# First layer's attention scores of two query tiles in one pass, with the rotary high-by-low products as 64-row halves

## The chip, the cores and the metric

The kernel runs on one core of a Trainium2 chip. Five engines work side by side from queues of their own: PE (TensorE, matrix products; PEld is its weight side), DVE (VectorE), ACT (ScalarE), POOL (GpSimd) and SP, which mostly issues DMAs. The metric is the device time of one execution in microseconds (us), lower is better.

## What is computed

The reference is a trunk of two layers over 1024 latent and 256 context tokens of width 1024. The first layer's mixer, the one of interest, is multi-head latent attention with 8 heads. A head's query and key have 128 plain and 64 rotary elements, and the rotary key is one for all heads:

```python
def _block_attention(q, k, v, scale):
    ...
    def step(qi):
        s = jnp.einsum('bqhgd,bkhd->bhgqk', qi, k).astype(jnp.float32) * scale
        p = jax.nn.softmax(s, axis=-1).astype(v.dtype)
        return jnp.einsum('bhgqk,bkhd->bqhd', p, v)

def _mla_mixer(h, hc, w_dq, q_norm, w_uq, w_dkv, kv_norm, w_ukv, w_o, need_ctx):
    ...
    q = _mla_q(h, w_dq, q_norm, w_uq, rows, cols)
    k, v = _mla_kv(h, w_dkv, kv_norm, w_ukv, rows, cols)
    kc, vc = _mla_kv(hc, w_dkv, kv_norm, w_ukv, None, None)
    k_all = jnp.concatenate([kc, k], 1)
    v_all = jnp.concatenate([vc, v], 1)
    out = _block_attention(q[:, :, :, None], k_all, v_all, scale) @ w_o
    if need_ctx:
        qc = _mla_q(hc, w_dq, q_norm, w_uq, None, None)
        out_c = _block_attention(qc[:, :, :, None], kc, vc, scale) @ w_o
```

A layer norm, a dense MLP, neighbourhood attention as the second layer's mixer and another MLP follow; the change does not touch them.

## The kernel before

Each fp32 operand of a matrix product is kept as two parts, a high one in fp32r (a copy rounded to that type) and a low one, the remainder. A product is then three passes: high by high, high by low and low by high (`mm3`, lines 66 to 68).

Tokens are handled in tiles of 128; tiles 0 and 1 are the context. The keys stand in three groups `GR`, of 256, 512 and 512 columns. `p1b` computes the queries of all heads and stores them in DRAM. For the rotary part (`pe`) a PE transpose gives the 64 rotary rows twice, one copy below the other; ACT copies both to `qst` as the high part (L382), and DVE replaces rows 64 to 127 by the low part (L383). The rotary key `ck[g][b][:, 2, :]` also holds its 64 rows twice (b = 0 high, b = 1 low).

`attn0` goes through heads, and in a head through 5 pairs of query tiles. `softmax(h, t, ...)` makes the scores of one tile: for each key group five products into one PSUM bank, of 512 or 256 columns. L468, L469 and L472 are the plain part, L470 the rotary high key against both query parts at once over 128 rows, and L471 the low key in the same way. Then DVE copies the bank to `p` with a running maximum (L473), takes the maximum (L476), ACT makes the exponential (L478), DVE the reciprocal (L479), and DVE (odd tiles) or POOL (even tiles) scales (L480). `pv` handles the pair before: four PE transposes of `p` per two key tiles (L491), a split into `th` (ACT, L54) and `tl` (DVE, L55), and six products into `po`, which DVE copies out (L499). Pair 0 is the context and has one key group; pairs 1 to 4 have three.

Between the pairs stand pieces of other work: the next two heads' keys and values (`pj`, `pv`, lines 66 to 68) and the modulation products of the second layer (L155), which multiply with a 32-column weight in four column parts of the array side by side. PSUM has 8 banks: three with the tag "u" (`po`, projections, modulation), three "d" (scores), two "t" (transposes).

The calls in the code are not the order on the engines: a scheduler reorders each engine's instructions when the program is built, within the dependencies; PE then runs them strictly in that order. `issue_after` and `mark` only say behind which product a piece may come.

Of the kernel before, what the change touches and what calls it, by code (L numbers as in the profile page):

```python
# [10 lines left out]
F32 = mybir.dt.float32  # L11
F32R = mybir.dt.float32r
AF = mybir.ActivationFunctionType
# [5 lines left out]
P = 128  # L19
# [22 lines left out]
class Trunk:  # L42
# [304 lines left out]
    def p1b(self):  # L347
# [6 lines left out]
        with tc.tile_pool(name="p1b", bufs=1, reuse_waits="tile") as sp:  # L354

            def pe(hg):
                h, lo = self.wload(a["wuqp"][hg], [P, 4, 256], f"p{hg}")
                for g, (o, n) in enumerate(GR):
                    qr = []
                    for i in range(n // P):  # L360
                        t = o // P + i
                        sl = slice(i * P, (i + 1) * P)
                        pp = self.bank("u", f"pp{hg}{t}", (P, 256))
                        ch, cl = self.cq[g]
                        for k in range(4):
                            self.mm3(pp, ch[:, k, sl], cl[:, k, sl], h[:, k, :], lo[:, k, :], k == 0, k == 3)
                        r = sp.tile([P, 4, 2, 64], F32, tag="qr", bufs=8, name=f"qr{hg}{t}")
                        if g == 0:
                            nc.scalar.copy(r[:, :, 0, :], pp.rearrange("p (a b) -> p a b", b=64))
                        else:  # L370
                            x = sp.tile([P, 4, 64], F32, tag="qx", bufs=2, name=f"qx{hg}{t}")
                            nc.scalar.copy(x.rearrange("p a b -> p (a b)"), pp)
                            self.rope(sp, r[:, :, 0, :], x, t - 2, 4)
                        nc.vector.tensor_copy(r[:, :, 1, :], r[:, :, 0, :])
                        qr.append(r.rearrange("p a d b -> p a (d b)"))
                    for hh in range(4):
                        pt = self.bank("t", f"qt{hg}{g}{hh}", (P, 4, P))
                        for i in range(n // P):
                            nc.tensor.transpose(pt[:, i, :], qr[i][:, hh, :], self.ident)
                        st = sp.tile([P, 512], F32R, tag="qst", bufs=2, name=f"qst{hg}{g}{hh}")  # L380
                        pf = pt.rearrange("p a b -> p (a b)")[:, 0:n]
                        nc.scalar.copy(st[:, 0:n], pf)  # L382
                        nc.vector.tensor_tensor(st[64:128, 0:n], pf[64:128, :], self.f(st[64:128, 0:n]),  # L383
                                                op=ALU.subtract)
                        nc.scalar.dma_start(self.qs[hg * 4 + hh][g], self.f(st[:, 0:n]))

            def nope(pr):
# [19 lines left out]
    def attn0(self):  # L407
        nc, tc, a = self.nc, self.tc, self.a
        self.od = [self.dp.tile([P, H0, 256], F32, name=f"od{i}") for i in range(5)]
        with ExitStack() as es:  # L410
# [41 lines left out]
                nc.sync.dma_start(self.f(s[:, 0:n]), self.qs[h][g])  # L452
                return q, s

            def softmax(h, t, q, kt, gks):

                g, off = grp_of(t)
                qq, qst = q
                sl = slice(off, off + P)
                st = sp.tile([P, 6], F32, tag="st", bufs=8, name=f"st{h}{t}")  # L460
                p = sp.tile([P, NTOK], F32, tag="p", bufs=5, name=f"p{h}{t}")
                for i, gk in enumerate(gks):
                    o0, n = GR[gk]
                    o = self.bank("d", f"s{h}{t}{gk}")[:, 0:n]
                    kh, kl = kt[gk]
                    ph, pl = (x[:, 2, :] for x in self.ck[gk])
                    mm = nc.tensor.matmul
                    mm(o, lhsT=qq[:, 0, sl], rhs=kh, start=True, stop=False)  # L468
                    mm(o, lhsT=qq[:, 0, sl], rhs=kl, start=False, stop=False)  # L469
                    mm(o, lhsT=qst[:, sl], rhs=ph, start=False, stop=False)  # L470
                    mm(o, lhsT=qst[:, sl], rhs=pl, start=False, stop=False)  # L471
                    self.mark = mm(o, lhsT=qq[:, 1, sl], rhs=kh, start=False, stop=True)  # L472
                    nc.vector.tensor_scalar(p[:, o0:o0 + n], o, 1.0, None, op0=ALU.mult, op1=ALU.max,  # L473
                                            accum_out=st[:, i:i + 1])
                m = len(gks)
                nc.vector.tensor_reduce(st[:, 3:4], st[:, 0:m], axis=AX, op=ALU.max, negate=True)  # L476
                n = sum(GR[gk][1] for gk in gks)
                nc.scalar.activation(p[:, 0:n], p[:, 0:n], AF.Exp, bias=st[:, 3:4], accum_out=st[:, 4:5])  # L478
                nc.vector.reciprocal(st[:, 5:6], st[:, 4:5])  # L479
                (nc.vector.tensor_scalar(p[:, 0:n], p[:, 0:n], st[:, 5:6], None, op0=ALU.mult) if t % 2 else nc.gpsimd.tensor_tensor(p[:, 0:n], p[:, 0:n], st[:, 5:6].broadcast_to([P, n]), op=ALU.mult))  # L480
                return p

            def pv(h, h2, pair, ps_, nb, vs):
                po = self.bank("u", f"po{h}{pair}", (P, 256))
# [21 lines left out]
            for h in range(H0):  # L506
# [10 lines left out]
                    total = len(todo)  # L517
                qs_ = [load_q(h, g) for g in range(3)]
                for pair in range(5):
                    pl = [softmax(h, t, qs_[grp_of(t)[0]], ks[h2], [0] if pair == 0 else [0, 1, 2])  # L520
                          for t in (pair * 2, pair * 2 + 1)]
                    if pend is not None:
                        pv(*pend)
                    pend = (h, h2, pair, pl, 2 if pair == 0 else 10, vs)
# [916 lines left out]
```

## Time and profile before

| what | value |
|---|---|
| median of 3 runs | 3142.84 us (3138.31 to 3143.91) |
| time of the profiled execution | 3141.2 us |
| its span, first to last instruction | 3139.4 us |
| mean granted clock of TensorE | 0.984 of full speed |
| PE busy | 96% of the span |
| DVE, ACT, POOL busy | 57%, 39%, 34% |
| first layer's attention | about 265 to 747 us of the span |

Times in the views are us from the start of the span. A row of the timeline has the start, the length, the engine, the line of the kernel, the operation, output<-inputs and the shape; [x <- y] is idle time of the engine just before and what ended it. PE's records overlap, since products are pipelined: how fast it goes is read from the distance between two starts. Repeated instructions are merged into one row (x8).

### The profile page before, as it was taken

The page shows a single profiled execution, that of the slowest core. Times are in us where ns is not written, and L with a number is a line of the kernel's source. Part 1 is how long each engine was busy: PE and PEld are TensorE (multiplying, and loading weights), DVE is VectorE, ACT ScalarE, POOL GpSimd, SP SyncE. Part 2 cuts the span into 40 slices and gives each one's busy share as a digit, 9 for nine tenths or more (in the row PEclk, how much of TensorE's full clock was granted, in tenths as well). Part 3 has the DMA queues.
Part 4 walks back from the last instruction along what each step waited for, and adds up shares of the span by engine and source line. Part 5 has one row for each costly group of instructions (what it writes and reads, how often), then busy time and mean ns, then how long its engine had stood idle before and what let it go on. Part 6 is the DMA issues. An engine that isn't in the chain of part 4 may idle for free.

```text
span 3139.4 us, 42125 instructions
## 1 busy us (share of the span) xinstructions
PE 3023.0 (96%) x15894; PEld 2528.9 (81%) x15894; DVE 1776.4 (57%) x3619; ACT 1208.8 (39%) x2068; POOL 1077.1 (34%) x667
## 2 busy tenths in 40 slices
PE   8999999999989999999999999999988899999997
PEld 4798888888878888888887788888877788878886
DVE  4345665665656656422228777777757666632228
ACT  2234444444445444301002455555543555521101
POOL 3362111112124343462118522232324044455227
PEclk9999999999999999999999999999999999999998
DMA  8445333313524444774435111111124244476434
GB/s 331 157 153 185 127 114 113 122 35 99 180 77 157 149 148 141 261 248 148 133 114 183 66 46 45 43 45 46 39 82 163 103 157 163 165 271 231 145 114 168
DMA packets 205724, 429.22 MB, mean 137 GB/s; under 512 B 16896, under 2 KB 124544, under 8 KB 199760
## 3 DMA queue, kind: packets, MB, share of 16 engines
q1 hardware_dynamic: 151472, 296.97, 28.7%
q10 hardware_dynamic: 54048, 129.56, 10.5%
q8 instruction: 125, 2.05, 0.3%
q14 instruction: 79, 0.65, 0.1%
HBM read 298.50 MB, written 127.96 MB: 136 GB/s over the span
## 4 chain that ended last, share of the span: by engine, by line
PE 79%; DVE 7%; issue 5%; POOL 3%; DMA 3%; ACT 3%; SPq 0%; DVEq 0%; ACTq 0%; POOLq 0%
PE py L66 7%; PE py L67 7%; PE py L68 7%; PE nj L66 3%; PE nj L68 3%; PE nj L67 3%; PE sb L68 2%; PE sb L66 2%; PE sb L67 2%; PE pt L491 2%; PE sa L66 2%; PE mps L155 2%; PE sa L68 2%; PE sa L67 2%; PE sc L67 2%
## 5 line engine op out<-in xcount | busy, mean ns | idle before, releaser
L1085 DVE TENSOR_TENSOR y<-py,y 128x512 f32<-128x512 f32 x252 | 172.8, 690 | 443.7 <-PE py L68 443.7
L480 POOL TENSOR_TENSOR p<-p,st 128x1280 f32<-128x1280 f32 (+1 forms) x40 | 79.2, 1980 | 383.4 <-DVE st L479 277.8
L66 PE MATMUL nj<-hTa,whn 128*128 128x512 f32 (+1 forms) x512 | 201.4, 393 | 2.6 <-ACT njt L1125 2.6
L66 PE MATMUL py<-w2xh,ub 128*128 128x512 f32 x504 | 196.1, 389 | 0.0
L67 PE MATMUL py<-w2xl,ub 128*128 128x512 f32 x504 | 196.1, 389 | 0.0
L68 PE MATMUL py<-w2xh,ub 128*128 128x512 f32 x504 | 196.1, 389 | 0.0
L68 PE MATMUL nj<-hTa,wln 128*128 128x512 f32 (+1 forms) x512 | 189.2, 370 | 2.0 <-POOL wln L61 2.0
L67 PE MATMUL nj<-hTa,whn 128*128 128x512 f32 (+1 forms) x512 | 188.7, 369 | 0.0
L54 ACT CAST th<-pt 128x512 fp32r<-128x512 f32 x168 | 96.9, 586 | 164.7 <-PE pt L491 162.3
L473 DVE TENSOR_SCALAR_CACHE_REDUCE p<-s 128x512 f32<-128x512 f32 (+1 forms) x208 | 116.9, 584 | 60.2 <-PE pt L491 33.4
L55 DVE TENSOR_TENSOR tl<-pt,th 128x512 fp32r<-128x512 f32 x168 | 114.2, 687 | 61.0 <-ACT th L54 59.8
L61 POOL TENSOR_TENSOR wln<-rawn,whn 128x1024 fp32r<-128x1024 f32 x28 | 67.4, 2407 | 210.6 <-ACT whn L59 210.5
L1202 ACT ACTIVATE pp<-pp,nst 128x640 f32<-128x640 f32 (+1 forms) x128 | 102.9, 804 | 95.2 <-DVE nst L1200 94.8
L59 ACT CAST w2xh<-w2r 128x1024 fp32r<-128x1024 f32 x28 | 28.1, 1049 | 284.2 <-PE py L68 189.2
L66 PE MATMUL py<-w2th,ub 128*128 128x512 f32 x324 | 126.7, 392 | 4.1 <-DVE y L1083 4.1
L68 PE MATMUL py<-w2th,ub 128*128 128x512 f32 x324 | 127.7, 394 | 0.0
L67 PE MATMUL py<-w2wl,ub 128*128 128x512 f32 x324 | 127.0, 392 | 0.0
L66 PE MATMUL py<-w2wh,ub 128*128 128x512 f32 x324 | 127.0, 392 | 0.0
L67 PE MATMUL py<-w2tl,ub 128*128 128x512 f32 x324 | 126.8, 391 | 0.0
L68 PE MATMUL py<-w2wh,ub 128*128 128x512 f32 x324 | 126.8, 391 | 0.0
L61 POOL TENSOR_TENSOR w2xl<-w2r,w2xh 128x1024 fp32r<-128x1024 f32 x28 | 67.2, 2420 | 172.9 <-ACT w2xh L59 172.9
L66 PE MATMUL py<-woh,oh 128*128 128x512 f32 x288 | 115.8, 403 | 10.2 <-DVE ty L671 9.1
(2133 smaller groups left out, 9508.3 us busy)
## 6 DMA issues: line engine op xcount, KB each, us to landing
ub<-ud SPq DMA_DIRECT2D x288, 256.0 KB
adaw<-in_ada_w SPq DMA_DIRECT2D x40, 1024.0 KB
w1r<-in_w SPq DMA_DIRECT2D x64, 512.0 KB
w2r<-in_mlp_w SPq DMA_DIRECT2D x64, 512.0 KB
ud<-uhld ACTq DMA_DIRECT2D x29, 512.0 KB
ud<-uhlc ACTq DMA_DIRECT2D x29, 512.0 KB
ud<-uhlb ACTq DMA_DIRECT2D x29, 512.0 KB
ud<-uhla ACTq DMA_DIRECT2D x28, 512.0 KB
```

What stands on the lines that cost most here:

```text
L54: nc.scalar.copy(hi, ps)
L55: nc.vector.tensor_tensor(lo, ps, self.f(hi), op=ALU.subtract)
L61: return h, e.tensor_tensor(lo, src, self.f(hi), op=ALU.subtract)
L66: mm(out, lhsT=ah, rhs=bh, start=first, stop=False, skip_group_check=more)
L67: mm(out, lhsT=ah, rhs=bl, start=False, stop=False, skip_group_check=more)
L68: return mm(out, lhsT=al, rhs=bh, start=False, stop=last, skip_group_check=more)
L155: nc.tensor.matmul(ps[32 * j:32 * j + 32, :], lhsT=self.sT[:, k, :], rhs=x, start=(k == 0), stop=(k == KD - 1), tile_position=(0, 32 * j))
L473: nc.vector.tensor_scalar(p[:, o0:o0 + n], o, 1.0, None, op0=ALU.mult, op1=ALU.max, accum_out=st[:, i:i + 1])
L480: (nc.vector.tensor_scalar(p[:, 0:n], p[:, 0:n], st[:, 5:6], None, op0=ALU.mult) if t % 2 else nc.gpsimd.tensor_tensor(p[:, 0:n], p[:, 0:n ...
L491: nc.tensor.transpose(pt[:, c, i, :], ps_[i][:, col:col + P], self.ident)
L1085: self.mark = nc.vector.tensor_tensor(y[t][:, ns], py, y[t][:, ns], op=ALU.add)
L1202: nc.scalar.activation(pp[:, 0:n], pp[:, 0:n], AF.Exp, bias=st[:, 2:3], accum_out=st[:, 3:4])
```

## The change

Four things are done. The scores of both tiles of a pair are made in one call, `softmax(h, pair, ...)`, all products ahead of all evictions. In `p1b`, `qst` is laid out by tile: even tiles keep the high part in rows 0 to 63 and the low one in 64 to 127, odd tiles have them the other way round; for that the subtraction becomes two DVE instructions, one for each half of the rows. For the two key groups of 512 columns the product with the low rotary key is no longer taken over 128 rows (both query parts) but over the 64 rows that hold the query's high part: rows 0 to 63 for the even tile and 64 to 127 for the odd one (the low-by-low term is left out there). These half products stand at the end, the even and the odd tile's one after the other. The group of 256 columns keeps its product over 128 rows. And the banks: both tiles' scores of the small group share one "d" bank, those of the second group take two "u" banks, those of the third two "d" banks.

In the changed kernel the score products are L475 (was L468), L476 (L469), L477 (L470), L479 (L471, small group alone), L480 (L472) and the half products L487; the transposes of `pv` are L512 (L491).

```diff
--- before.py
+++ after.py
@@ -380,8 +380,10 @@
                         st = sp.tile([P, 512], F32R, tag="qst", bufs=2, name=f"qst{hg}{g}{hh}")
                         pf = pt.rearrange("p a b -> p (a b)")[:, 0:n]
                         nc.scalar.copy(st[:, 0:n], pf)
-                        nc.vector.tensor_tensor(st[64:128, 0:n], pf[64:128, :], self.f(st[64:128, 0:n]),
-                                                op=ALU.subtract)
+
+                        for i, d in enumerate((slice(64, 128), slice(0, 64))):
+                            x, v = (z[d, 0:n].rearrange("p (a u q) -> p a u q", u=2, q=P)[:, :, i, :] for z in (pf, st))
+                            nc.vector.tensor_tensor(v, x, self.f(v), op=ALU.subtract)
                         nc.scalar.dma_start(self.qs[hg * 4 + hh][g], self.f(st[:, 0:n]))
 
             def nope(pr):
@@ -452,33 +454,52 @@
                 nc.sync.dma_start(self.f(s[:, 0:n]), self.qs[h][g])
                 return q, s
 
-            def softmax(h, t, q, kt, gks):
-
-                g, off = grp_of(t)
+            def softmax(h, pair, q, kt, gks):
+
                 qq, qst = q
-                sl = slice(off, off + P)
-                st = sp.tile([P, 6], F32, tag="st", bufs=8, name=f"st{h}{t}")
-                p = sp.tile([P, NTOK], F32, tag="p", bufs=5, name=f"p{h}{t}")
-                for i, gk in enumerate(gks):
-                    o0, n = GR[gk]
-                    o = self.bank("d", f"s{h}{t}{gk}")[:, 0:n]
+                mm = nc.tensor.matmul
+                ts = (pair * 2, pair * 2 + 1)
+                sls = [slice(o, o + P) for o in (grp_of(t)[1] for t in ts)]
+                sts = [sp.tile([P, 6], F32, tag="st", bufs=8, name=f"st{h}{t}") for t in ts]
+                ps = [sp.tile([P, NTOK], F32, tag="p", bufs=5, name=f"p{h}{t}") for t in ts]
+                hf = (slice(0, 64), slice(64, 128))
+                outs = {}
+                for gk in gks:
+                    n = GR[gk][1]
                     kh, kl = kt[gk]
                     ph, pl = (x[:, 2, :] for x in self.ck[gk])
-                    mm = nc.tensor.matmul
-                    mm(o, lhsT=qq[:, 0, sl], rhs=kh, start=True, stop=False)
-                    mm(o, lhsT=qq[:, 0, sl], rhs=kl, start=False, stop=False)
-                    mm(o, lhsT=qst[:, sl], rhs=ph, start=False, stop=False)
-                    mm(o, lhsT=qst[:, sl], rhs=pl, start=False, stop=False)
-                    self.mark = mm(o, lhsT=qq[:, 1, sl], rhs=kh, start=False, stop=True)
-                    nc.vector.tensor_scalar(p[:, o0:o0 + n], o, 1.0, None, op0=ALU.mult, op1=ALU.max,
-                                            accum_out=st[:, i:i + 1])
-                m = len(gks)
-                nc.vector.tensor_reduce(st[:, 3:4], st[:, 0:m], axis=AX, op=ALU.max, negate=True)
+                    if gk == 0:
+                        b = self.bank("d", f"s{h}{pair}0", (P, 2, 256))
+                    for i, sl in enumerate(sls):
+                        o = outs[gk, i] = b[:, i] if gk == 0 else self.bank("ud"[gk % 2], f"s{h}{pair}{gk}{i}")[:, 0:n]
+                        mm(o, lhsT=qq[:, 0, sl], rhs=kh, start=True, stop=False)
+                        mm(o, lhsT=qq[:, 0, sl], rhs=kl, start=False, stop=False)
+                        mm(o, lhsT=qst[:, sl], rhs=ph, start=False, stop=False)
+                        if gk == 0:
+                            mm(o, lhsT=qst[:, sl], rhs=pl, start=False, stop=False)
+                        self.mark = mm(o, lhsT=qq[:, 1, sl], rhs=kh, start=False, stop=gk == 0)
+
+
+                for gk in gks:
+                    if gk:
+                        pl = self.ck[gk][1][:, 2, :]
+                        for i, sl in enumerate(sls):
+                            self.mark = mm(outs[gk, i], lhsT=qst[hf[i], sl], rhs=pl[hf[i], :], start=False, stop=True)
+                for gk in gks:
+                    o0, n = GR[gk]
+                    for i in range(2):
+                        nc.vector.tensor_scalar(ps[i][:, o0:o0 + n], outs[gk, i], 1.0, None, op0=ALU.mult, op1=ALU.max,
+                                                accum_out=sts[i][:, gk:gk + 1])
                 n = sum(GR[gk][1] for gk in gks)
-                nc.scalar.activation(p[:, 0:n], p[:, 0:n], AF.Exp, bias=st[:, 3:4], accum_out=st[:, 4:5])
-                nc.vector.reciprocal(st[:, 5:6], st[:, 4:5])
-                (nc.vector.tensor_scalar(p[:, 0:n], p[:, 0:n], st[:, 5:6], None, op0=ALU.mult) if t % 2 else nc.gpsimd.tensor_tensor(p[:, 0:n], p[:, 0:n], st[:, 5:6].broadcast_to([P, n]), op=ALU.mult))
-                return p
+                for t, p, st in zip(ts, ps, sts):
+                    nc.vector.tensor_reduce(st[:, 3:4], st[:, 0:len(gks)], axis=AX, op=ALU.max, negate=True)
+                    nc.scalar.activation(p[:, 0:n], p[:, 0:n], AF.Exp, bias=st[:, 3:4], accum_out=st[:, 4:5])
+                    nc.vector.reciprocal(st[:, 5:6], st[:, 4:5])
+                    if t % 2:
+                        nc.vector.tensor_scalar(p[:, 0:n], p[:, 0:n], st[:, 5:6], None, op0=ALU.mult)
+                    else:
+                        nc.gpsimd.tensor_tensor(p[:, 0:n], p[:, 0:n], st[:, 5:6].broadcast_to([P, n]), op=ALU.mult)
+                return ps
 
             def pv(h, h2, pair, ps_, nb, vs):
                 po = self.bank("u", f"po{h}{pair}", (P, 256))
@@ -517,8 +538,7 @@
                     total = len(todo)
                 qs_ = [load_q(h, g) for g in range(3)]
                 for pair in range(5):
-                    pl = [softmax(h, t, qs_[grp_of(t)[0]], ks[h2], [0] if pair == 0 else [0, 1, 2])
-                          for t in (pair * 2, pair * 2 + 1)]
+                    pl = softmax(h, pair, qs_[grp_of(pair * 2)[0]], ks[h2], [0] if pair == 0 else [0, 1, 2])
                     if pend is not None:
                         pv(*pend)
                     pend = (h, h2, pair, pl, 2 if pair == 0 else 10, vs)
```

What the scheduler makes of it, on PE in mid-attention, head 3. Names: `s` and its digits are a score bank (head, then tile and group before; head, pair, group and tile of the pair after), `kh`, `kl` the key's parts, `q` and `qs` the query's plain and rotary parts, `ck10` and `ck11` the rotary key of group 1, high and low; an output is followed by what streams, then by what is held as the weights or the other way round. Before, tile 8 and the first 512-column group:

```order
L66 MATMUL po31_5070<-th318_5136,vh18_3879 128x256
L468 MATMUL s381_5347<-kh111_4259,q32_4778 128x512
L469 MATMUL s381_5347<-kl111_4260,q32_4778 128x512
L470 MATMUL s381_5347<-ck10_107,qs32_4780 128x512
L471 MATMUL s381_5347<-ck11_108,qs32_4780 128x512
L472 MATMUL s381_5347<-kh111_4259,q32_4778 128x512
L468 MATMUL s382_5354<-kh112_4270,q32_4778 128x512
L469 MATMUL s382_5354<-kl112_4271,q32_4778 128x512
```

All of these are products over 128 rows. The changed kernel, the same group of tiles 8 and 9 (pair 4):

```order
L475 MATMUL s3410_5358<-kh111_4271,q32_4787 128x512
L476 MATMUL s3410_5358<-kl111_4272,q32_4787 128x512
L477 MATMUL s3410_5358<-ck10_107,qs32_4789 128x512
L480 MATMUL s3410_5358<-kh111_4271,q32_4787 128x512
L487 MATMUL s3410_5358<-ck11_108,qs32_4789 128x512
L66 MATMUL po31_5076<-th318_5142,vh18_3894 128x256
L475 MATMUL s3411_5363<-kh111_4271,q32_4787 128x512
L476 MATMUL s3411_5363<-kl111_4272,q32_4787 128x512
L477 MATMUL s3411_5363<-ck10_107,qs32_4789 128x512
L480 MATMUL s3411_5363<-kh111_4271,q32_4787 128x512
L487 MATMUL s3411_5363<-ck11_108,qs32_4789 128x512
L67 MATMUL po31_5076<-tl318_5143,vh18_3894 128x256
```

The low rotary product has moved to the end of its bank's five, and the even tile's (rows 0 to 63) and the odd tile's (rows 64 to 127) are apart, with five products over 128 rows in between. Later in the same pair, the last half product stands right ahead of the modulation products:

```order
L475 MATMUL s3421_5373<-kh112_4282,q32_4787 128x512
L476 MATMUL s3421_5373<-kl112_4283,q32_4787 128x512
L477 MATMUL s3421_5373<-ck20_109,qs32_4789 128x512
L480 MATMUL s3421_5373<-kh112_4282,q32_4787 128x512
L487 MATMUL s3421_5373<-ck21_110,qs32_4789 128x512
L155 MATMUL mps110_4772<-adaw115_5475,sT_80 32x512 x4
L155 MATMUL mps110_4772<-adaw116_5614,sT_80 32x512 x4
L512 MATMUL pt336_5442<-ident_73,p36_5185 128x128
```

Here two loads of modulation weights are used in one stretch, and PE goes from the half product to them and from them to transposes over 128 rows. In head 2 two half products of a pair do follow each other:

```order
L68 MATMUL pj112_4284<-ck20_109,wlkv1_2761 128x512
L477 MATMUL s2311_4479<-ck10_107,qs22_4076 128x512
L480 MATMUL s2311_4479<-kh101_3049,q22_4074 128x512
L487 MATMUL s2310_4474<-ck11_108,qs22_4076 128x512
L487 MATMUL s2311_4479<-ck11_108,qs22_4076 128x512
L512 MATMUL pt214_4383<-ident_73,p22_4201 128x128
L512 MATMUL pt214_4383<-ident_73,p23_4202 128x128
```

The even tile's half product waited there until the odd tile's other products were done.

## Rows read from the trace of the kernel before

**Rows 1.** The page: busy time of PE; the chain that ended last, by engine.

```profile
PE 3023.0 (96%) x15894; PEld 2528.9 (81%) x15894; DVE 1776.4 (57%) x3619; ACT 1208.8 (39%) x2068; POOL 1077.1 (34%) x667
PE 79%; DVE 7%; issue 5%; POOL 3%; DMA 3%; ACT 3%; SPq 0%; DVEq 0%; ACTq 0%; POOLq 0%
```

**Rows 2.** Three stretches: start:end, length, busy (x instructions) PE, PEld, DVE, ACT, POOL, clock.

```profile
150.00:265.00 115.00, 113.86 (x749) 103.75 (x748) 52.89 (x97) 44.95 (x100) 55.04 (x82) 1.00 0.52 189
400.00:520.00 120.00, 119.02 (x808) 100.47 (x807) 75.20 (x223) 53.96 (x96) 21.31 (x11) 1.00 0.36 121
736.00:747.00 11.00, 7.61 (x32) 6.84 (x31) 9.34 (x17) 7.02 (x9) 4.60 (x3) 0.69 0.61 203
```

**Rows 3.** Waits of PE from 265 to 747 us: total, times, longest.

```profile
PE po L67 <- DVE st L476: 3.4, 1, 3.4
PE po L67 <- DVE tl L55: 2.0, 9, 0.3
...
PE po L66 <- ACT th L54: 0.9, 3, 0.3
```

**Rows 4.** Timeline of PE, products of 512 and 256 columns in a row.

```profile
509.20 0.40 PE L470 MATMUL s<-ck,qs 128*128 128x512 f32 x1
509.44 0.39 PE L471 MATMUL s<-ck,qs 128*128 128x512 f32 x1
...
509.89 0.28 PE L66 MATMUL po<-th,vh 128*128 128x256 f32 x1
510.01 0.28 PE L67 MATMUL po<-tl,vh 128*128 128x256 f32 x1
```

**Rows 5.** Timeline of PE around one group of modulation products.

```profile
504.54 0.28 PE L471 MATMUL s<-ck,qs 128*128 128x256 f32 x1
504.66 0.28 PE L472 MATMUL s<-kh,q 128*128 128x256 f32 x1
504.87 1.06 PE L155 MATMUL mps<-adaw,sT 128*32 128x512 f32 x8
505.86 0.39 PE L468 MATMUL s<-kh,q 128*128 128x256 f32 x1
506.09 0.28 PE L469 MATMUL s<-kl,q 128*128 128x256 f32 x1
```

**Rows 6.** Timeline of PE's weight loads at the same place.

```profile
504.54 0.19 PEld L472 LDWEIGHTS s<-kh,q 128*128 128x128 f32 x1
504.87 0.16 PEld L155 LDWEIGHTS mps<-adaw,sT 128*32 128x32 f32 x8
505.86 0.19 PEld L468 LDWEIGHTS s<-kh,q 128*128 128x128 f32 x1 [0.84 <-DVE st L479]
```

**Rows 7.** Line L155 from 280 to 700 us: what ended its idle time.

```profile
issue: 7.0, 23
```

**Rows 8.** Groups by line and shape, 280 to 740 us, the softmax chain.

```profile
L478 ACT ACTIVATE p<-p,st 128x1280 f32<-128x1280 f32 x61 | 83.4, 1366 | 65.3 <-DVE st L476 65.3
L473 DVE TENSOR_SCALAR_CACHE_REDUCE p<-s 128x512 f32<-128x512 f32 x124 | 83.2, 686 | 11.5 <-PE s L472 10.6
L480 POOL TENSOR_TENSOR p<-p,st 128x1280 f32<-128x1280 f32 x31 | 72.0, 2322 | 304.1 <-DVE st L479 219.8 <-PE pt L491 38.4 <-PE s L472 31.7
L480 DVE TENSOR_SCALAR p<-p,st 128x1280 f32<-128x1280 f32 x30 | 26.5, 884 | 0.7
L499 DVE COPY o<-po 128x256 f32<-128x256 f32 x37 | 15.5, 420 | 11.4 <-PE po L68 11.2
```

**Rows 9.** Timeline of PE at the end of the stage.

```profile
739.52 0.58 PE L67 MATMUL po<-tl,vh 128*128 128x256 f32 x1 [3.39 <-DVE st L476]
739.90 0.41 PE L68 MATMUL po<-th,vl 128*128 128x256 f32 x1
740.11 0.41 PE L66 MATMUL po<-th,vh 128*128 128x256 f32 x1
```

**Rows 10.** Line L383: lengths in ns (least, middle, most) and shapes.

```profile
L383 DVE TENSOR_TENSOR qst<-qt,qst x24: 420/687/696, 174.2 to 245.6; 64x512 fp32r<-64x512 f32 x16, 64x256 fp32r<-64x256 f32 x8
```

## The prediction

> **What bounds the kernel now.** I read the page first: TensorE is busy for 96% of the span and holds 79% of the chain that ended last [rows 1]. A share over the whole span says little of one stage, so next I cut out the stages that the change touches [rows 2]: the projections of the first layer's queries (up to about 265 us) and its attention (265 to 747 us). In a stretch of 120 us in mid-attention PE is busy for 119.02, DVE for 75.20, ACT for 53.96, and the granted clock is 1.00, the higher level of 2.4 GHz. So PE is the limit of this stage, and the waits say how tight: over all of it PE stood still for 3.4 us in one place, for 2.0 in nine short waits for `tl` and for 0.9 in three for `th` [rows 3]. What the change takes from PE's instruction stream, or puts into it, therefore arrives almost whole at the end of the stage, and nothing behind the stage waits for a time that is fixed.
>
> PE's records overlap, so I take prices from the distance between starts, not from lengths. A product of 512 columns takes 0.23 us so (three from 509.20 to 509.89), one of 256 columns 0.12, although their records are 0.39 and 0.28 long [rows 4]. The weights of the next product are fetched meanwhile: the load for L472 starts at 504.54, together with the product of L471 before it [rows 5, 6].
>
> **What the change removes and adds.** The operands are the same and so is the number of products. Per head there are 4 pairs of tiles with two 512-column key groups each, so 8 x 4 x 2 x 2 = 128 high-by-low rotary products become products over 64 rows. Two of them, one in each half of the array's rows, can run side by side. If all 64 couples did, 64 x 0.23 = 14.7 us would go. That is the most that the change can give, and it needs the two halves of a couple to follow each other.
>
> In the order of the changed kernel they do not. Counted over all of PE's attention, the 128 products stand in 114 stretches: 102 are a single product between products of 128 rows (or, 16 of them, right before an L155 group), 11 are couples, one is four in a row. The scheduler put the other query tile's work, transposes and `po` products between the halves. A lone half saves nothing: it streams the same 512 columns in the same 0.23 us. So the couples give little, and the question is what 114 changes between 128 rows and 64 rows cost.
>
> No run here shows that with products before and after it. The nearest row is L155, the modulation products, which use the array in four parts of 32 columns. Around it three things are seen. Going in: L472 starts at 504.66 and L155 at 504.87, 0.21 apart where 0.12 is the rule, so 0.09 us more [rows 5]. Coming out: the record of L155 ends at 505.93; ordinary records reach 0.16 past the next start, so the next product should start at 505.77 and starts at 505.86, again 0.09. And its weights are not fetched ahead: load and product of L468 both start at 505.86, and L469 follows after 0.23 instead of 0.12, so 0.11 more [rows 5, 6]. Together 0.29 us per visit. The weight side's idle time says the same: 7.0 us in 23 cases that wait for nothing shown, 0.30 each [rows 7].
>
> I take this price for a change of rows too; the lower end is nothing. For a half product the load on the way in is 128 weights wide, not 32, so it costs 0.11 there as well: 0.09 + 0.11 + 0.09 + 0.11 = 0.40 us on top of its 0.23. Then:
> - 86 lone products between 128-row work: 86 x 0.40 = 34.4 us.
> - 16 lone products right before L155: the way out is L155's way in, so 16 x (0.09 + 0.11) = 3.2 us.
> - 11 couples: the second's weights come 0.11 behind the first's, so a couple takes 0.11 + 0.23 = 0.34 instead of 0.46, and 0.40 - 0.12 = 0.28 is left; 3.1 us.
> - the four in a row: 3 x 0.11 + 0.23 = 0.56 instead of 0.92, against 0.40: nothing.
> - L155 itself is visited in 22 stretches where 30 were counted: 8 x 0.29 = 2.3 us less.
>
> That is 40.7 - 2.3 = 38.4 us more on PE; the upper end, 0.40 for each of the 114 and nothing saved by couples, is 45.6 - 2.3 = 43.3. A slower PE gives the others more time: of the 2.9 us that PE waits for `tl` and `th` [rows 3] I take half away. Sum: +37 us on this execution's 3141.2 us, so 3178. The median of the three runs is 3142.84, 1.6 above this execution, so I say 3179.
>
> The Trainium skill states the rule behind this: "TensorEngine Tiling (Array Packing)", Key Properties, says that changing the tiling mode, not merely the tile, drains the engine. The L155 rows agree for parts of 32 columns (0.09 us on either side); for halves of 64 rows no run here shows it.
>
> **Edits that I cost at nothing.** The `qst` subtraction becomes two DVE instructions of half the columns, 24 more in all. A 64x512 one takes 0.69 us and a 64x256 one 0.42 [rows 10], so 16 are dearer by 0.15 and the rest by less: under 4 us of DVE, in a stretch where DVE is busy for 52.89 of 115 [rows 2]. Without that cover it costs those 4 us.
>
> The evictions (L473, 0.69 us for 512 columns) now come after all products of a pair, two score tiles share one bank, and two of the pair's banks come from the group that `po`, `pj` and `pv` use. What is late next would be the softmax chain: eviction 0.69, exponential 1.37 and the scaling, 0.88 on DVE or 2.32 on POOL [rows 8], so 2.9 us for odd tiles and 4.4 for even ones, plus two one-column instructions and the waits in DVE's queue. I added up the distances over the rows of the order: from a pair's last score product to the first transpose of its probabilities the least is 5.0 us for odd and 6.5 for even tiles (before: mostly above 9). That is still cover for one more eviction in the queue, and every change of mode makes it longer. The `po` bank is worse off: in 4 of 37 cases less than 1.5 us of PE work stands before its next use, with a copy of 0.42 in between [rows 8]. I take nothing; the upper bound is some ten pairs stalled by 1 us, +10.
>
> At the end of the stage PE stands still for 3.39 us behind DVE, which is splitting the next weights, and then runs at the lower clock: products of 256 columns are 0.21 apart instead of 0.12, in a stretch with a mean granted clock of 0.69 [rows 2, 9]. The order there is nearly the same in both kernels, so I leave it; it can move the time by about 5 us either way.
>
> **The rivals.**
> 1. *A change of rows is free* (not slower). Rows 0 to 63 are a part of the same array, all 128 columns stay in use, and the trace shows a price only for columns. Then the 13 couples save between 0.12 and 0.23 us each, 1.6 to 3.0, and L155 2.3: 3141.2 - 4 to 5 = 3136 to 3137, and with some of the stalls above 3142. For it speaks that nothing in the trace has shown a price for rows. It decides from 0.03 us per stretch downward, since 114 x 0.03 eats these 4 us.
> 2. *Only the drain, with the weights still fetched ahead*: 0.18 for a lone half, 0.09 before L155. 86 x 0.18 + 16 x 0.09 + 11 x 0.06 - 2.3 = 15.3, so 3156. Against it: in [rows 6] the load waits as long as the product.
> 3. *No price for rows, but the tighter banks and the shorter distance to the transposes stall PE*: up to +10 - 4, so 3147. Against it speaks the cover counted above.
>
> **How the numbers follow.** Full price 0.64, with its own range of 3168 to 3188 (stalls, the stage's end); drain alone 0.12; free 0.19; stalls 0.05. The range of 3138 to 3188 takes in the first two and the part of rival 1 with some stalls. About 0.2%, 6 us, is what a measurement of this kernel can tell from no change. Slower by more than that: the first two cases, 0.76; within it: most of rivals 1 and 3, 0.17; faster: 0.07.
>
> **What would show it.** In the profile after, L487 (the half products) should start 0.32 us or more after an L480 of 512 columns, with its load starting no earlier than itself, and the next product's load should also wait; PE's weight side should show some 110 more idle cases put down to nothing, of 0.2 to 0.4 us. In the couple of head 2 the two L487 should start 0.11 apart. If L487 starts 0.23 behind L480 and its load with L480's start, the price is nothing and rival 1 holds. Waits of PE for the scores' evictions of more than 5 us would speak for rival 3. The prediction fails if the clock falls in the stage, or if a half product streams at another rate than 0.23.

## The result and the profile after

The changed kernel takes 3180.28 us (median of 4 runs, 3179.19 to 3181.57) against 3142.29 for the kernel before (3138.31 to 3143.91): ratio 1.0125, 95% interval 1.0113 to 1.0137. The profiled execution took 3179.19, its span is 3177.4 and the mean granted clock 0.985. Forecast were 3179.0 and slower.

The page after, the two lines that answer to [rows 1]:

```profile
PE 3056.2 (96%) x15894; PEld 2517.7 (79%) x15894; DVE 1790.6 (56%) x3643; ACT 1208.1 (38%) x2068; POOL 1076.8 (34%) x667
PE 78%; DVE 7%; issue 4%; POOL 3%; ACT 3%; DMA 3%; SPq 0%; ACTq 0%; DVEq 0%; POOLq 0%
```

PE has the same 15894 products and is busy for 33.2 us longer; no other engine takes over. So the loss is in PE's stream. The stretches of [rows 2] after the change, the last one at the new end of the stage, with the same columns:

```profile
150.00:265.00 115.00, 112.95 (x730) 102.89 (x729) 53.59 (x117) 43.70 (x96) 54.52 (x81) 0.99 0.53 190
400.00:520.00 120.00, 118.23 (x728) 90.28 (x727) 70.65 (x202) 47.81 (x84) 19.87 (x10) 0.99 0.31 104
770.00:781.00 11.00, 5.50 (x28) 4.94 (x28) 9.80 (x17) 6.98 (x11) 5.63 (x3) 0.84 0.60 189
```

In mid-attention PE is as busy as before, at nearly the same clock, but does 728 products in 120 us where it did 808. Its weight side, which [rows 2] shows at 100.47 us busy, is at 90.28: it waits more. Where, the timeline says. PE first, then the weight loads at the same place:

```profile
420.76 0.40 PE L480 MATMUL s<-kh,q 128*128 128x512 f32 x1
421.09 0.50 PE L487 MATMUL s<-ck,qs 64*128 64x512 f32 x1
421.52 0.39 PE L475 MATMUL s<-kh,q 128*128 128x256 f32 x1
421.75 0.28 PE L476 MATMUL s<-kl,q 128*128 128x256 f32 x1
...
423.52 0.40 PE L480 MATMUL s<-kh,q 128*128 128x512 f32 x1
423.85 0.49 PE L487 MATMUL s<-ck,qs 64*128 64x512 f32 x1
424.27 1.06 PE L155 MATMUL mps<-adaw,sT 128*32 128x512 f32 x6
425.26 0.66 PE L512 MATMUL pt<-ident,p 128*128 128x128 f32 x4
425.84 1.04 PE L155 MATMUL mps<-adaw,sT 128*32 128x512 f32 x2
426.82 0.39 PE L66 MATMUL po<-th,vh 128*128 128x256 f32 x1
```

```profile
420.54 0.19 PEld L480 LDWEIGHTS s<-kh,q 128*128 128x128 f32 x1
421.09 0.18 PEld L487 LDWEIGHTS s<-ck,qs 64*128 64x128 f32 x1 [0.36 <-issue]
421.52 0.19 PEld L475 LDWEIGHTS s<-kh,q 128*128 128x128 f32 x1 [0.25 <-issue]
421.63 0.19 PEld L476 LDWEIGHTS s<-kl,q 128*128 128x128 f32 x1
```

This is the forecast picture. The half product (64x512) starts 0.33 behind L480 instead of 0.23, its load starts with it instead of one product earlier, and the next product comes 0.43 later, its load again no earlier than itself, and is followed after 0.23 instead of 0.12. From L480's start to L476's are 0.99; without changes of mode it would be 0.23 + 0.23 + 0.12 = 0.58. The difference is 0.41, forecast was 0.40. Over all 86 lone halves, worked out from starts in this way, the middle one costs 0.393 and all together 33.3 us. The view of line L487 counts the same on the weight side: what ended its idle time, then how long in all and how often:

```profile
  issue: 40.1, 113
```

Forecast were some 110 such cases of 0.2 to 0.4 each; here are 113, 0.35 on average.

Waits of PE from 265 to 790 us, which answer to [rows 3]:

```profile
PE po L67 <- DVE st L495: 4.0, 1, 4.0
PE po L67 <- DVE tl L55: 3.6, 6, 1.8
PE po L66 <- ACT th L54: 2.7, 4, 1.5
```

No wait for a score's eviction is among them. `tl` and `th` have grown from 2.9 to 6.3, while PE has become slower.

Taken apart, the span is 38.0 longer (3177.4 - 3139.4): from the first score product to the last, start to start, 499.4 against 465.6 us, +33.8; from there to the stage's last `po` product 49.9 against 47.5, +2.4; the rest of the program, which is the same, +1.7 (rounded). A better end of the stage for later comparisons is the last product of the attention's output projection (480 products `py`, lines 66 to 68), since up to there every kernel has done the same work: 639.8 against 603.8, +36.0.

### The profile page after: what moved, and what is told of

It is laid out like the page before. It is cut to its first block, busy times and chain, and to the rows that moved or that the text cites. A ratio compares the mean times of both kernels' runs of the same rounds, so it can differ in the third digit from the quotient of the medians.

```text
span 3177.4 us, 42177 instructions
## 1 busy us (share of the span) xinstructions
PE 3056.2 (96%) x15894; PEld 2517.7 (79%) x15894; DVE 1790.6 (56%) x3643; ACT 1208.1 (38%) x2068; POOL 1076.8 (34%) x667
## 4 chain that ended last, share of the span: by engine, by line
PE 78%; DVE 7%; issue 4%; POOL 3%; ACT 3%; DMA 3%; SPq 0%; ACTq 0%; DVEq 0%; POOLq 0%
PE py L66 7%; PE py L68 7%; PE py L67 7%; PE nj L66 3%; PE nj L68 3%; PE nj L67 3%; PE sb L66 2%; PE sb L68 2%; PE sb L67 2%; PE pt L512 2%; PE sa L66 2%; PE sa L68 2%; PE sa L67 2%; PE sc L67 2%; PE sc L66 2%
## 5 line engine op out<-in xcount | busy, mean ns | idle before, releaser
L67 PE MATMUL py<-w2xl,ub 128*128 128x512 f32 x504 | 196.1, 389 | 0.0
L67 PE MATMUL nj<-hTa,whn 128*128 128x512 f32 (+1 forms) x512 | 188.9, 369 | 0.0
L491 DVE TENSOR_SCALAR_CACHE_REDUCE p<-s 128x512 f32<-128x512 f32 (+1 forms) x208 | 116.6, 585 | 68.6 <-PE s L487 46.2
L496 ACT ACTIVATE p<-p,st 128x1280 f32<-128x1280 f32 (+1 forms) x80 | 95.5, 1194 | 83.7 <-DVE st L495 73.4
L67 PE MATMUL py<-w2wl,ub 128*128 128x512 f32 x324 | 127.1, 392 | 0.0
L67 PE MATMUL py<-w2tl,ub 128*128 128x512 f32 x324 | 127.0, 392 | 0.0
```

The costliest lines, as they stand in the source:

```text
L67: mm(out, lhsT=ah, rhs=bl, start=False, stop=False, skip_group_check=more)
L491: nc.vector.tensor_scalar(ps[i][:, o0:o0 + n], outs[gk, i], 1.0, None, op0=ALU.mult, op1=ALU.max, accum_out=sts[i][:, gk:gk + 1])
```

## The experiments

In the diffs a + line is new against the kernel that the text names. Each run's ratio is to the kernel before on the same chip, with its 95% interval.

**Do the halves cost it?** The changed kernel with the late products over all 128 rows again (which adds the low-by-low term back); PE's order of products is the same:

```diff
-  self.mark = mm(outs[gk, i], lhsT=qst[hf[i], sl], rhs=pl[hf[i], :], start=False, stop=True)
+  self.mark = mm(outs[gk, i], lhsT=qst[:, sl], rhs=pl, start=False, stop=True)
```

> The changed kernel with one thing undone: the late rotary products take all 128 rows again (high-by-low and low-by-low, as before the change); their places, the banks, the late evictions and the qst layout stay, and the order on every place of PE is the same. Theory (the changes between 128 and 64 rows cost all of it): the 114 stretches' extra of about 0.39 us (0.12 for couples) goes, so 3180 - 38 = 3142 us, 3139 to 3145. Rival (the late evictions, the shared banks and the shorter distance to the transposes cost it): 3165 us or more.

Measured: 3146.16 us (ratio 1.0013, 1.0005 to 1.0022). 34.1 of the 38.0 us go with the halves. But 4 us stay that should not be there, beyond the expected 3139 to 3145: the rest of the change is not free. That is taken up below.

**Price of a change of rows, and of fewer rows.** The kernel before, where only L471 is cut, for the two large key groups: to rows 0 to 63, and in a second kernel to rows 0 to 95. Both leave out part of the scores' rotary term; the order stays that of before, so every one of the 128 products is alone.

```diff
-                    mm(o, lhsT=qst[:, sl], rhs=pl, start=False, stop=False)
+                    r = slice(0, 64 if gk else P)
+                    mm(o, lhsT=qst[r, sl], rhs=pl[r, :], start=False, stop=False)
```

> The kernel before, with one thing changed: for the two groups of 512 columns L471 takes only rows 0 to 63 (high-by-low; the low-by-low term is left out). Order, banks and layout stay as before; each of the 128 products stands alone between products over 128 rows. Theory: 128 x 0.39 = 50 us more than before, 3192 us, 3187 to 3196. Rival (the restructuring costs, not the rows): 3142 us.

> As the run with 64 rows in the kernel before, but over rows 0 to 95 (high-by-low and half of the low-by-low term); a product of 96 rows still uses the array as one part of 128 rows. Theory (the price is for changing how the array is divided): no price, 3142 us, 3139 to 3145. Rival (any product that uses fewer rows than its neighbours waits for them and fetches its weights late): 50 us more, 3192.

Measured: with 64 rows 3191.66 us (1.0157, 1.0141 to 1.0172), with 96 rows 3142.07 (1.0, 0.9991 to 1.0009). 49.2 us for 128 visits is 0.385 each, with none of the change's other edits in it. With 64 rows (L472 there) PE's timeline has the pattern of the changed kernel:

```profile
505.42 0.39 PE L469 MATMUL s<-kl,q 128*128 128x512 f32 x1
505.64 0.40 PE L470 MATMUL s<-ck,qs 128*128 128x512 f32 x1
505.97 0.50 PE L472 MATMUL s<-ck,qs 64*128 64x512 f32 x1
506.40 0.50 PE L473 MATMUL s<-kh,q 128*128 128x512 f32 x1
506.83 1.06 PE L155 MATMUL mps<-adaw,sT 128*32 128x512 f32 x6
```

With 96 rows the view of L472 shows no idle time on the weight side; with 64 rows it shows 44.3 us in 124 cases. So it is not the smaller operand that costs, but passing from the whole array to a half of it and back. That is the rule of the Trainium skill ("TensorEngine Tiling (Array Packing)", Key Properties: a changed tiling mode drains the engine) that the prediction had only seen at L155; these runs agree for halves of 64 rows and put 0.385 us on it.

**Do halves that follow each other pay?** In the changed kernel a pair's four halves are kept together, behind all its other scores, and the next pair's scores behind them (32 stretches of four, 16 of them right before L155):

```diff
+                with self.tc.issue_after(self.mark.ins), self.tc.high_priority(200):
                     for gk in gks:
...
+                                 self.half = self.mark = mm(outs[gk, i], lhsT=qst[hf[i], sl], rhs=pl[hf[i], :], start=False, stop=True)
```

> The changed kernel with the four half products of a pair held together: they are queued behind the last of the pair's other products, with a raised priority, and a pair's first product behind the halves of the pair before; key and value pieces are held back to the end of a head's pairs so that the banks suffice. 32 stretches of four, 16 of them right before L155. Theory (price per change of division, halves of a couple side by side): a stretch of four took 0.11 us less in the changed kernel than four products of 128 rows, and 0.2 less again where L155 follows; 32 x 0.11 + 16 x 0.2 = 6.7 us below the same order with 128 rows. If five open banks cost no stall, 3135 us, 3131 to 3140. Rival (holding five banks and strict order between pairs stalls PE): over 3145 us.

The same, but in 64 couples, each behind the scores of its key group:

> The same, but held together only by couples (each key group's two halves): 64 stretches of two, 16 of them right before L155. Theory: a couple costs 0.12 us more than two products of 128 rows, 0.08 less right before L155, so 48 x 0.12 - 16 x 0.08 = 4.5 us, less 3 us for fewer stretches of L155 (19 instead of 30): 3144 us, 3140 to 3149. If the loads of a couple's halves were serial (0.28 per couple, as predicted): 3152.

And, as the control of the fours, their order with 128 rows:

> The run with fours, the late products over all 128 rows, same order on PE. Theory: 3142 us or, with 26 stretches of L155 instead of 30, 3141; it is the base from which the halves' own worth in the run with fours is read: 5 to 8 us. If the halves in fours are worth nothing, both times are the same. Rival (strict order stalls): both over 3145 us.

Measured: fours 3145.68 (1.0012, 1.0003 to 1.0021), couples 3152.41 (1.0034, 1.0021 to 1.0048), control 3145.38 (1.0009, 1.0 to 1.0018). Keeping the halves together brings back nearly all that single ones cost. On PE the fours do save: the timeline of the kernel with fours (its halves are L491)

```profile
422.36 0.39 PE L485 MATMUL s<-kh,q 128*128 128x512 f32 x1
422.68 0.73 PE L491 MATMUL s<-ck,qs 64*128 64x512 f32 x4
423.34 0.39 PE L66 MATMUL po<-th,vh 128*128 128x256 f32 x1
423.56 0.28 PE L67 MATMUL po<-tl,vh 128*128 128x256 f32 x1
```

goes from L485 to L67 in 1.20 us, where four full products would need 0.23 + 4 x 0.23 + 0.12 = 1.27. Over all 32, more where L155 follows, that comes to 5.0 us. From the first score product to the last output projection the fours take 607.2 us, the control 608.9: only 1.7 shorter. PE's waits for `tl` and `th`, first with fours and then in the control, show part of where it went:

```profile
PE po L67 <- DVE tl L55: 4.0, 10, 1.0
PE po L66 <- ACT th L54: 1.2, 3, 0.6
```

```profile
PE po L67 <- DVE tl L55: 2.8, 9, 1.0
PE po L66 <- ACT th L54: 0.6, 2, 0.3
```

That is 1.8 us. The medians show no gain at all, and the runs of each of the two lie some 6 us apart. The expectations were missed by 10 us with fours and by 4 in the control; both lie over 3145, where the rival put them (strict order and held banks stall PE). All waits of PE up to the last output projection sum to 16.2 us with fours and 13.7 in the control, against 6.8 before. So the 4 us belong to what the two share: the new arrangement of the scores or the strict order, which these two runs do not tell apart. The couples missed their expectation by 8 us and hit the number that it gave for loads one after the other. Their trace does not bear that out: the two halves of a couple and their loads start 3 to 4 ns apart, and a couple costs 0.16 us (middle of the 48 that L155 does not follow). What is longer there is PE's waits, 14.6 us.

**What is L155 worth?** The prediction gave 2.3 us for 22 stretches of L155 instead of 30. The fence of the changed kernel above holds a hint that was overlooked: a step of the modulation product, four parts of 32 columns side by side, was split there, six instructions at 424.27 and two at 425.84. The six take 0.99 to the next start and the two 0.98; [rows 5] has 0.99 for eight. A part of a step streams as long as the whole. To test it, the kernel before with the four products of a step raised in priority together, which leaves 21 stretches and splits no step:

```diff
+            with self.tc.high_priority(600):
                 for j, x in enumerate(parts):
                     nc.tensor.matmul(ps[32 * j:32 * j + 32, :], lhsT=self.sT[:, k, :], rhs=x, ...)
```

> The kernel before, with the modulation products (L155) given a raised priority, so that the four column parts of a step stay together: 21 stretches during the attention instead of 30, nothing left out. Theory (0.29 us for each visit to the divided array, columns as rows): 9 x 0.29 = 2.6 us less, 3139.5 us, 3136 to 3142. Rival (what the split steps cost was hidden, or the displaced products stall PE elsewhere): 3142 us or more.

Measured: 3134.65 (0.9974, 0.9964 to 0.9985), and once more later, beside the next run:

> The kernel before with the L155 products raised in priority, once more, beside the kernel above on the same chip: 3132 to 3137 if its lead of 8 us over the kernel before repeats; 3142 if the lead was chance.

3133.07 (0.9971, 0.996 to 0.9983). That is 7 to 8 us, not 2.6. The time that L155 takes on PE can be had from starts: from the product ahead of a stretch to the second product behind it, less the ordinary steps of those two. The sum is 38.6 us over the 30 stretches before, 27.5 over the 21 here, and 30.0 over the 22 of the changed kernel's order with full rows. On PE, then, raising the priority takes away 11.1 us, and some 9 of them arrive at the last output projection (603.8 before; 594.8 and 594.4 in the two profiles of this kernel). In the same way fewer stretches took 8.6 us off PE in the change, not 2.3.

**What do the other edits cost?** If L155 gave 8.6, the first run above should have been at 3134, and was at 3146. The changed kernel with full rows and L155 together, beside the run just told:

> The changed kernel with its products of the high rows over all 128 rows, and with the L155 products raised in priority as in the run that set them together: no change of rows is left, and L155 stands in 19 stretches. The full-row version measured 3146.16 with 22 such stretches, the kernel before with its 21 measured 3134.65. Theory: four scores in one bank with late evictions cost about 10 us by themselves, and in the changed kernel the fewer L155 stretches hid that; then this kernel comes to 3143 to 3146, some 10 above the next kernel of this call. Rival: the new arrangement of the scores is free, and what set the full-row version apart lies elsewhere; then it comes to 3133 to 3136, level with the next kernel.

Measured: 3137.48 (0.9988, 0.9979 to 0.9997), 4.4 us above its neighbour. The arrangement costs something here too, but less than the 10 expected. In the profiles with this arrangement one thing stood out that none with the scores tile by tile has. DVE's scaling of an odd tile, 0.88 us in [rows 8], is in the changed kernel (280 to 775 us)

```profile
L499 DVE TENSOR_SCALAR p<-p,st 128x1280 f32<-128x1280 f32 x31 | 32.5, 1049 | 0.8
```

and single ones are much longer. From the timeline of the changed kernel, DVE, POOL, and PE behind them:

```profile
495.00 1.79 DVE L499 TENSOR_SCALAR p<-p,st 128x1280 f32<-128x1280 f32 x1
496.72 1.28 DVE L55 TENSOR_TENSOR tl<-pt,th 128x512 fp32r<-128x512 f32 x2
```

```profile
493.80 2.32 POOL L501 TENSOR_TENSOR p<-p,st 128x1280 f32<-128x1280 f32 x1 [10.77 <-DVE st L497]
```

```profile
497.45 0.38 PE L67 MATMUL po<-tl,vh 128*128 128x256 f32 x1 [1.77 <-DVE tl L55]
...
499.11 0.42 PE L67 MATMUL po<-tl,vh 128*128 128x256 f32 x1
499.33 0.42 PE L68 MATMUL po<-th,vl 128*128 128x256 f32 x1
```

POOL scales the even tile until 496.12, and DVE's scaling beside it ends 0.67 later. Eight of 32 are longer than 1.1 us here, nine in each of the two kernels with full rows and 27 with fours; most of the long ones last 0.68 us and the time that POOL's ran beside them. With both tiles' scores made together, their scalings now fall together. `tl` comes late, PE waits 1.77 us, and behind the wait products of 256 columns are 0.22 apart: the granted clock is at its lower level of 1.2 GHz for a while (0.83 on average from 495 to 505 us). The Trainium skill ("SBUF — State Buffer", SBUF: two separate sides) says that DVE and POOL share a pair of ports that one of them locks for a whole instruction; these lengths agree. Was this the price? All scalings on DVE, in the kernel just told and, as a control, in its neighbour:

```diff
-                    if t % 2:
-                        nc.vector.tensor_scalar(p[:, 0:n], p[:, 0:n], st[:, 5:6], None, op0=ALU.mult)
-                    else:
-                        nc.gpsimd.tensor_tensor(p[:, 0:n], p[:, 0:n], st[:, 5:6].broadcast_to([P, n]), op=ALU.mult)
+                    nc.vector.tensor_scalar(p[:, 0:n], p[:, 0:n], st[:, 5:6], None, op0=ALU.mult)
```

> The run before last (four scores a pass, full rows, L155 together: 3137.48) with the scaling of even tiles on DVE as well, so that POOL has no part in the softmax. In the profiles with the scores in one pass nine or ten of the 32 long DVE scalings took 1.11 to 2.51 us instead of 0.88, each longer by about as much as POOL's own scaling ran beside it, and PE waited 1.8 us for tl behind one of them and then lost clock; with the scores tile by tile none was longer than 0.89. Theory, collision: that is most of the 4.4 us between this arrangement and the kernel before with L155 together (3133.07); then no scaling is over 0.9, PE's waits for tl and th fall by 3 to 5 us, and the time comes to 3133 to 3135. Rival, banks and late evictions: the price stays, 3137 to 3139, as DVE also gets 32 scalings of 0.88 more.

> The control: the kernel before with L155 together (3133.07) and the scaling of even tiles on DVE. No scaling collides there, so by either theory nothing is to be had: 3132 to 3135. If it falls by as much as the run above, taking POOL out helps for another reason than the collision.

Measured: 3136.26 (0.9976, 0.9964 to 0.9987), and the control 3126.17 (0.994, 0.9927 to 0.9952). The theory of the collision falls: no scaling is longer than 0.89 us now, and yet the waits of PE for `tl` and `th` are where they were, and the time is lower by about 0.1% only, between what the theory and its rival gave. From the first score to the last output projection both kernels take 598.6 us. The scalings of the run (least, middle and most in ns; the 345 is of 256 columns), then PE's waits from 255 to 800 us, and those of the kernel with POOL from 265 to 800:

```profile
L499 DVE TENSOR_SCALAR p<-p,st x80: 345/886/890, 269.2 to 734.9; 128x1280 f32<-128x1280 f32 x64, 128x256 f32<-128x256 f32 x16
```

```profile
PE po L67 <- DVE tl L55: 4.6, 7, 1.0
PE po L66 <- ACT th L54: 3.3, 5, 1.9
```

```profile
PE po L67 <- DVE tl L55: 4.8, 7, 1.8
PE po L67 <- DVE st L496: 4.0, 1, 4.0
PE po L66 <- ACT th L54: 3.1, 4, 1.9
```

The control, where nothing collided, fell more, 6 us below what was expected of it. Its profile does not show the gain in the attention: from the first score to the last output projection it takes 595.1 us against 594.4 in its neighbour with POOL. (Its last `po` product comes 5 us earlier behind the last score, but only because 83 output projections stand before it instead of 112.) It is the rest of the program, behind the stage, that is shorter, 2263.2 us against 2268.9, and there the two kernels do the same work; so what made the control faster is not shown.

The price of the arrangement is there all the same, in every pair of kernels that differ in it and little else. In the table, "stage" is the time from the first score product to the last output projection, L155's time is worked out as above, "waits" is all that PE waits in the stage, and the price is the difference of stages less that of L155:

| kernels without and with the new arrangement (full rows) | stage | L155 | waits | price |
|---|---|---|---|---|
| before; changed with full rows | 603.8; 603.7 | 38.6; 30.0 | 6.8; 11.8 | 8.5 |
| L155 together; the same | 594.4; 598.6 | 27.5; 26.6 | 8.0; 12.3 | 5.1 |
| and all scalings on DVE; the same | 595.1; 598.6 | 27.4; 26.7 | 8.3; 11.0 | 4.2 |

So it is 4 to 9 us, read from one profile of each kernel, and over half of it is longer waits of PE, in the first two pairs above all for `th` and `tl`. In the second pair, for one, the kernel without the arrangement has

```profile
PE po L67 <- DVE st L477: 3.4, 1, 3.4
PE po L67 <- DVE tl L55: 2.7, 11, 0.3
PE po L66 <- ACT th L54: 0.9, 3, 0.3
```

where the one with it has the 4.0, 4.8 and 3.1 shown above. The medians of the whole time, with the same 0.7 to 8.6 us for L155, would give 5 to 12; what of that lies outside the stage was not traced.

Last, fours, L155 together and all scalings on DVE at once:

> The halves in fours (3145.68 when measured alone), L155 raised in priority (23 stretches) and all scalings on DVE. From the run of fours: L155 in 23 stretches and 23 pieces instead of 26 and 27, about 4 us; the collision, 3 to 5; and if the 5 us that the fours save on PE come through without it, the time is 3128 to 3133. If the fours' saving is lost to waits again, 3135 to 3139.

Measured: 3131.95 (0.9954, 0.9941 to 0.9967), within the first range. It is 4.3 us below the kernel with full rows and the same scalings (3136.26), where the fours' 5.0 less 1.5 for L155 (28.2 us against 26.7) would give 3.5. The intervals of the two overlap, and in the profiles the stage is only 0.7 shorter (597.9 against 598.6), with 1.8 us more of waits; whether the saving comes through stays open. The fastest kernel of all is the control: the scores tile by tile as before, L155 together, no scaling on POOL, 3126.17 us, faster than the kernel before the change and the one after it.

## Why the prediction came out right, and where it did not

The time (3179.0 against 3180.28) and the cause are right. That the time fits to about 1 us is luck: two errors of the sum, of 6 us each, cancel in it. (Added up without rounding, the forecast's terms give 3179.8.)

- **86 lone products, 0.40 each:** 0.393 measured, 33.3 us instead of 34.4. Both parts of the price, the late start and the load that is not fetched ahead, are as the prediction took them over from L155. The 64-row cut alone gives 0.385.
- **16 before L155, 0.20 each:** 0.20 measured.
- **11 couples, 0.28 each:** mis-sized. The step "the second's weights come 0.11 behind the first's" failed. In PE's timeline of the changed kernel the couple in head 2 reads

```profile
418.39 0.39 PE L480 MATMUL s<-kh,q 128*128 128x512 f32 x1
418.71 0.50 PE L487 MATMUL s<-ck,qs 64*128 64x512 f32 x2
419.14 1.09 PE L512 MATMUL pt<-ident,p 128*128 128x128 f32 x8
```

  and the two halves take no longer than one: 0.43 to the next start, as the lone one at 421.09. They start 3 to 4 ns apart, and so do their loads. A couple costs 0.16, together 1.7 us instead of 3.1.
- **The four in a row, nothing:** it gains 0.11.
- **L155, 8 stretches at 0.29:** mis-sized, 8.6 us instead of 2.3. The sum priced visits and overlooked that a split step streams twice.
- **Edits at nothing:** this step failed. The late evictions, the shared banks and the pairs in step together cost 4 to 9 us, within the bound of +10 that the prediction named, and not where it looked: no wait for an eviction of a score is in the profile, but those for `th` and `tl` are longer. At the stage's end, where the prediction left the order out of account, PE waits 1.5 us for `th` and then 4.0, where it was 3.4 in one wait. The longer `qst` work is not it: the 48 subtractions of line L386 have a median of 0.417 us, and [rows 2] and the stretch up to 265 us after differ by 0.7 us of DVE. "I take half away" of the waits for `tl` and `th` failed as well: they grew.

With the measured terms: 33.3 + 3.2 + 1.7 - 0.1 - 8.6 = 29.5 on PE, and 36.0 between the first score and the last output projection; the 6.5 between them lie inside the 4 to 9 of the table, so they can be the arrangement's price.

Rival 1 (rows are free) and rival 2 (loads fetched ahead) are excluded by the 64-row cut; rival 3 had a true core, some 4 to 9 us of its own, though not a change of rows without a price. What stays open is how that price divides among banks, order and the softmax chain: no kernel changed these one at a time.

## What to carry to other kernels

Products on a half of the array can pay only if the order really puts them side by side: count, in the order on the engine, how often the array's division changes, and price each change from any row that already shows one. Price products that run side by side by streams, not by visits: a group that a scheduler tears apart streams once per piece. And when the sum of the terms hits the total, check the terms one by one: here a saving and a cost that were both missed cancelled.

## What was unexpected of the hardware

- A lone product over 64 rows amid products over 128 costs 0.385 to 0.39 us more than one over 128 (128 visits in one kernel, 86 in the other); cutting a product to 96 rows costs nothing and saves nothing (ratio 1.0).
- Two loads into different row halves go side by side, as the products do: in the kernel with fours the products of one stretch start at 0, 3, 335 and 337 ns, their loads at 0, 3, 108 and 112.
- A DVE scaling of 128x1280 that meets POOL's took 1.79 us instead of 0.88 (at most 3.02, with fours), though the two touch different tiles.
- A wait of 1.77 us in a stage that is otherwise at 2.4 GHz was followed by products at the 1.2 GHz pace.
